# A hybrid Hyena and mLSTM encoder block on one core: where split weights lie, when pools are handed on, and what stands ahead of the first products

## The chip, the cores and the metric

The kernel runs on one core of a Trainium2 chip. The metric is device time in microseconds from launch to end, lower is better; the time before is the median of three runs, 2859.32 us (2859.23 to 2859.35).

## The reference, cut to what matters

All arrays are float32; L = 512 tokens, D = 2048, feed-forward width 5632.

```python
hn = rmsnorm(x, norm1_w)
proj = hn @ w_in                      # 2048 x 11280
conv_out = depthwise_conv3(proj[..., :5120])
y_a = hyena(conv_out[..., :3072])     # two long convolutions with learned filters
y_b = o * (mlstm_forward + mlstm_backward)
gate_a, gate_b = sigmoid(proj's last 4096 columns)      # "merge"
mixed = gate_a * (y_a @ w_branch_a) + gate_b * (y_b @ w_branch_b)
x = x + mixed @ w_out
gu = rmsnorm(x, norm2_w) @ w_gate_up  # 2048 x 11264
x = x + (silu(gu[..., :5632]) * gu[..., 5632:]) @ w_down
return rmsnorm(x, norm_f_w)
```

## The kernel before, in words

Every float32 operand of a product is split into two fp32r tiles, a high part (a cast on ScalarE) and the rest (a subtraction on VectorE). `mm3` (L78) makes one product of three TensorE instructions: high by high, high by rest, rest by high. A weight tile is the stationary operand in most stages.

Stages, in order of time: load and transpose x and the first column group of w_in (L302 to L348, to about 40 us); the other columns of w_in, with Hyena and mLSTM as a side stream between them (to 818 us); the merge gates (818 to 1138 us); branch a and branch b (to 1313 us); w_out (to 1495 us); gate_up (to 2376 us); down (to the end).

Merge and gate_up use one level of Strassen and Winograd (class `Winograd`, L1095): 256 columns are made by seven products with 256-column moving operands, over eight pairs of k blocks. `load` brings four raw tiles, `add` makes the eight sums s1 to s4, `split` the high and low tiles (14 splits for 256 columns, each used for four pairs, so by 12 instructions). Merge makes 16 such groups, gate_up 44. In merge the moving operands are the X blocks (pool `ap`) and their combinations T (pool `ts`); in gate_up all are T tiles (`tp`, `ta`, `tb`).

Merge's split weights go through a ring of six high and six low tiles: four in `wp` (names `wh`, `wl` in the trace) and two on the right side (`h`, `l`); its sums through six right-hand tiles. gate_up's go through five and five: four in `wp`, one in `h2` and `l2`. Laid out by the pools' sizes, the tiles of `wp`, the X blocks, `ts`, `h2` and `l2` start at multiples of 256 bytes; merge's right-hand `h` and `l` start 32 bytes below such a multiple, and all T tiles of gate_up 32 bytes above one (`shifted`, L58, is there for such offsets).

At the end of w_out the last 256 columns (`out_group(3, 1)`) are run to their end (L1410), then the pool `ap`, which holds the operand of w_out, is left (L1411), and the pools of gate_up take its place. The T tiles of pair 6 (`combos(b_a, ...)`, L1430) and the first products stand behind that in the code. gate_up's first group takes products 1 and 2 over pairs 0 to 6, then calls `late`, which transposes the last output columns and makes pair 7 from them (L1148 to L1156).

An x block is transposed on TensorE and split (L315 to L328). The first w_in tile is loaded after the first piece of x (L308 to L312). The side stream is made of generators: `hyena(q)` fetches its inputs when it starts (L833 to L835), unless the step before it has done so; `mlstm` does that only for a following `mlstm` (L974). In branch a, y_b and o are loaded by the SP queue (L1306). In down, the four first h tiles take the place of T tiles (`hpa`, L1463), and all raw h loads are issued ahead through three tiles (L1468).

The order of instructions on each engine is made by a planner, which goes by the order of the code, by what is ready and by estimated costs, so it is near the order of the code but not the same. Weight loads go through the SP queue.

```python
    def mm3(o, aH, aL, bH, bL, start, stop):
        mm(o, aH, bH, start, False)
        mm(o, aH, bL, False, False)
        mm(o, aL, bH, False, stop)
```

Of the kernel before, what the change touches and what calls it, by code (L numbers as in the profile page):

```python
# [8 lines left out]
F32 = mybir.dt.float32  # L9
# [25 lines left out]
def hybrid_block_kernel(ctx, tc, x, norm1_w, w_in, conv_w, conv_b, filt_w1, filt_b1, filt_freq1,  # L35
# [27 lines left out]
    ap_cm = tc.tile_pool(name="ap", bufs=32)  # L63
    ap = ap_cm.__enter__()
# [18 lines left out]
    def split(pool, tag, src, shape=(P, L)):  # L83
        h = new(pool, tag, shape, F32R)
        l = new(pool, tag, shape, F32R)
# [221 lines left out]
    raws = []  # L307
    for c, (c0, n) in enumerate(pieces):  # L308
        for tb in range(4):
            nc.sync.dma_start(xt[c][tb], x2d[tb * P:(tb + 1) * P, c0:c0 + n])  # L310
        if c in (0, 2, 3):
            raws.append(load_a(w_in, len(raws) * L, 0))  # L312
    first_group = group_feat(w_in, 0, KB, 0, X, raws)

    def x_block(kb):  # L315
# [3 lines left out]
        for tb in range(4):  # L319
            nc.tensor.transpose(ps[:, tb * P:(tb + 1) * P], xt[c][tb][:, k0:k0 + P], ident)  # L320
        return ps

    def x_split(kb, ps):
        h = new(ap, "a", dt=F32R)
        l = new(ap, "a", dt=F32R)
# [3 lines left out]

    for kb in range(0, KB, 2):  # L330
# [557 lines left out]
    def mlstm(h, following=None):  # L888
# [122 lines left out]
    def stream_a():  # L1011
        yield from gate_rows()
        yield from need("filter")
        for kind, n in (("hy", 0), ("hy", 1), ("hd", 0), ("hy", 2), ("hy", 3)):
            yield from hyena(n) if kind == "hy" else mlstm(n)
# [3 lines left out]
        for h in (1, 2, 3):  # L1019
            yield from mlstm(h, h + 1)  # L1020
# [74 lines left out]
    class Winograd:  # L1095
# [30 lines left out]
        def cols(self, c0, psf, loaded=None, after={}, late=None):  # L1126
# [35 lines left out]
            product(p3, s4, "22")  # L1162
# [64 lines left out]
    wm_cm = {t: tc.tile_pool(name="wm" + t, bufs=b, side="right", reuse_waits="tile") for t, b in (("r", 4), ("s", 6), ("h", 2), ("l", 2))}  # L1227
# [7 lines left out]
    def ring(tag, shape, dt, own, pool, extra, more):  # L1235
# [9 lines left out]

    merge = Winograd(
        w_in, XT, ring("wr", (P, 4, 256), F32, 3, wm["r"], "r", 4),
        ring("wh", (P, 4, P), F32R, 4, wm["h"], "h", 2), ring("wl", (P, 4, P), F32R, 4, wm["l"], "l", 2),
        lambda: new(wm["s"], "s", (P, 4, P)), xo, lambda: bt((P, 256)))
# [8 lines left out]
    def load_ya():  # L1258
        for b in range(8):
            ya.append(split(ap, "a", load_tile(d_ya, b, nc.gpsimd)))  # L1260
# [11 lines left out]
    for t in ("l", "h", "s", "r"):  # L1272
# [14 lines left out]
    def branch_a():  # L1287
# [3 lines left out]
        def put_yb():  # L1291
            t, o = raw.pop(0)
            nc.vector.tensor_tensor(t, t, o, ALU.mult)
            yb.append(split(py, "y", t))

        for g in range(8):
# [9 lines left out]
            raw.append((load_tile(d_yb, g, nc.sync), load_tile(d_o, g, nc.sync)))  # L1306
# [298 lines left out]
```

## Time and profile before

| what | value |
|---|---|
| median of three runs | 2859.32 us |
| the profiled execution's own time | 2869.02 us |
| its span, first to last instruction | 2867.3 us |
| TensorE (PE) busy | 2840.8 us, 99% |
| VectorE (DVE) busy | 2104.9 us, 73% |
| ScalarE (ACT) busy | 1273.0 us, 44% |
| GpSimd (POOL) busy | 186.2 us, 6% |

Busy means that at least one instruction of the engine was running. TensorE's instructions overlap: a product of 256 columns is shown as 0.28 us long, while the next one starts some 0.12 us later. The pace of a stretch is therefore read from the starts, or from the count of instructions in a window. In a tile's name, `T,wh` is the moving operand T with the stationary operand wh.

### The profile page before, as it was taken

Reading aid. Unit: us, or ns where it says so; the run is one execution under the profiler, and the core shown is the slowest. Engines: PE = TensorE matmul, PEld = TensorE weight load, DVE = VectorE, ACT = ScalarE, POOL = GpSimd, SP = SyncE. Lnnn points to the kernel's source line nnn. Section 1 sums busy time; section 2 is a strip of 40 time slices with the busy share of each in tenths; the row PEclk is TensorE's granted clock in tenths of the full one; section 3 lists DMA queues with packets and bytes.
Section 4 is the critical chain, followed back from the end, with each engine's and each line's share of the span. In section 5 each row is a group of like instructions: output and inputs, shape, how many; then the busy total and the mean of one; then the engine's idle time right before and its main releaser. Section 6 shows DMA issues by size and latency. Waiting matters only on the chain.

```text
span 2867.3 us, 47431 instructions
## 1 busy us (share of the span) xinstructions
PE 2840.8 (99%) x18028; PEld 2569.3 (90%) x18028; DVE 2104.9 (73%) x3844; ACT 1273.0 (44%) x2259; POOL 186.2 (6%) x431
## 2 busy tenths in 40 slices
PE   9999999999999999999999999999999999999998
PEld 7888878888899999888899999999999998888886
DVE  6898869888588888554459889888898885233336
ACT  5434453446645545223445444444444445233224
POOL 0101121012100001000010000000000000000000
PEclk9999999999999999999999999999999999999999
DMA  5334443344344445643443343334333336343433
GB/s 180 115 118 129 125 133 122 110 144 147 114 151 129 133 140 164 223 140 109 136 142 118 124 127 122 115 115 128 124 118 118 120 102 217 96 129 115 126 115 126
DMA packets 281490, 376.97 MB, mean 131 GB/s; under 512 B 18620, under 2 KB 214660, under 8 KB 281261
## 3 DMA queue, kind: packets, MB, share of 16 engines
q1 hardware_dynamic: 257243, 298.36, 34.0%
q0 software_dynamic: 22752, 73.44, 7.6%
q8 instruction: 141, 2.31, 0.3%
q10 hardware_dynamic: 1266, 2.13, 0.2%
q14 instruction: 88, 0.72, 0.1%
HBM read 326.67 MB, written 47.20 MB: 130 GB/s over the span
## 4 chain that ended last, share of the span: by engine, by line
PE 71%; DVE 1%; DMA 0%; ACT 0%; issue 0%; ACTq 0%
PE mm L76 50%; PE sd L76 21%; DMA wr<-in_w_down_dram 0%; PE sd L1364 0%; DVE h L87 0%; DVE T L1392 0%; DVE s L1122 0%; ACT h L86 0%; DVE wl L177 0%; DVE wl L1106 0%; PE sd L998 0%; DVE x L1532 0%; ACT sq L1535 0%; ACT x L1544 0%; DVE g L957 0%
## 5 line engine op out<-in xcount | busy, mean ns | idle before, releaser
L177 DVE TENSOR_TENSOR wl<-wr,wh 128x512 fp32r<-128x512 f32 x512 | 350.8, 689 | 452.8 <-ACT wh L176 444.7
L176 ACT CAST wh<-wr 128x512 fp32r<-128x512 f32 x512 | 316.7, 622 | 739.1 <-PE mm L76 674.3
L76 PE MATMUL mm<-a,wh 128*128 128x512 f32 (+1 forms) x2128 | 620.8, 375 | 0.4 <-ACT wh L176 0.4
L76 PEld LDWEIGHTS mm<-a,wh 128*128 128x128 f32 x2128 | 386.1, 189 | 67.5 <-ACT wh L176 0.8
L76 PE MATMUL mm<-T,wh 128*128 128x256 f32 x2232 | 401.2, 282 | 2.8 <-ACT T L1391 2.3
L76 PE MATMUL mm<-a,wl 128*128 128x512 f32 (+1 forms) x1064 | 398.2, 374 | 1.0 <-DVE wl L177 1.0
L76 PE MATMUL sd<-T,wh 128*128 128x256 f32 x2224 | 397.6, 281 | 0.0
L76 PE MATMUL mm<-wh,h 128*128 128x512 f32 x1280 | 394.7, 389 | 1.1 <-ACT h L86 1.1
L76 PEld LDWEIGHTS mm<-T,wh 128*128 128x128 f32 x2232 | 341.7, 189 | 3.4 <-ACT T L1391 2.5
L1105 ACT CAST wh<-s 128x512 fp32r<-128x512 f32 x365 | 226.8, 622 | 253.3 <-PE sd L76 123.5
L76 PEld LDWEIGHTS sd<-T,wh 128*128 128x128 f32 x2224 | 339.1, 188 | 0.0
L76 PE MATMUL mm<-T,wl 128*128 128x256 f32 x1116 | 311.8, 279 | 0.3 <-DVE wl L1106 0.3
L76 PE MATMUL sd<-T,wl 128*128 128x256 f32 x1112 | 310.0, 279 | 0.0
L76 PEld LDWEIGHTS mm<-wh,h 128*128 128x128 f32 x1280 | 240.3, 188 | 51.3 <-ACT h L86 1.3
L1106 DVE TENSOR_TENSOR wl<-s,wh 128x512 fp32r<-128x512 f32 x365 | 249.9, 686 | 11.5 <-ACT wh L1105 8.1
L76 PE MATMUL mm<-wl,h 128*128 128x512 f32 x640 | 249.1, 389 | 0.0
L76 PE MATMUL mm<-wh,a 128*128 128x512 f32 (+1 forms) x896 | 247.2, 360 | 0.0
L76 PEld LDWEIGHTS mm<-a,wl 128*128 128x128 f32 x1064 | 201.0, 189 | 35.8 <-DVE wl L177 1.4
L76 PEld LDWEIGHTS mm<-T,wl 128*128 128x128 f32 x1116 | 211.1, 189 | 0.5 <-DVE wl L1106 0.5
L76 PEld LDWEIGHTS sd<-T,wl 128*128 128x128 f32 x1112 | 209.8, 189 | 0.0
L76 PEld LDWEIGHTS mm<-wh,a 128*128 128x128 f32 x896 | 160.3, 189 | 24.6
L76 PE MATMUL mm<-wl,a 128*128 128x512 f32 (+1 forms) x448 | 161.0, 359 | 0.0
(368 smaller groups left out, 4776.3 us busy)
## 6 DMA issues: line engine op xcount, KB each, us to landing
wr<-in_w_in_dram SPq DMA_DIRECT2D x140, 512.0 KB, 3.6
r<-in_w_gate_up_dram SPq DMA_DIRECT2D x100, 512.0 KB, 4.6
wr<-in_w_down_dram SPq DMA_DIRECT2D x88, 512.0 KB, 3.7
wr<-in_w_gate_up_dram SPq DMA_DIRECT2D x76, 512.0 KB, 4.2
r<-in_w_in_dram SPq DMA_DIRECT2D x36, 512.0 KB, 4.5
wr<-in_w_out_dram SPq DMA_DIRECT2D x32, 512.0 KB, 3.6
d_h<-xo POOLq DMA_DIRECT2D x44, 256.0 KB, 2.6
hl<-d_h SPq DMA_DIRECT2D x44, 256.0 KB, 3.5
```

What stands on the lines that cost most here:

```text
L76: nc.tensor.matmul(o, a, b, start=start, stop=stop)
L176: nc.scalar.copy(h, src)
L177: nc.vector.tensor_tensor(l, src, h.bitcast(F32), ALU.subtract)
L1105: nc.scalar.copy(h, a)
L1106: nc.vector.tensor_tensor(l, a, h.bitcast(F32), ALU.subtract)
```

## The change

- The X blocks, y_a and the operand of w_out lie in two pools of eight tiles, `al` and `ah`, in place of `ap`; a tile holds high and low part of one block. The blocks 0 to 7 of w_out's operand lie in `ah`, 8 to 15 in `al`.
- Start: the first w_in tile is loaded in two halves, behind the first and the second piece of x. Six unread products of ones are put ahead of the first transposes, and two and six unread transposes between those of block 1.
- `mlstm(0)` fetches the inputs of `hyena(2)` ahead.
- Merge: the first two splits of each kind take tiles of `wp`, all others rings of five right-hand tiles; the sums take the eight `wh` and `wl` tiles of `wp`.
- y_b and o are loaded by the POOL queue in branch a.
- End of w_out: after four of the eight steps of the last group `ah` is left, gate_up's `ta`, `tb`, `r2` and `h2` take its place, and pair 6 is made; then the group is ended. gate_up's sums, three of its raw tiles and one low tile lie in tiles of `al`.
- gate_up's first group: products 1, 2 and 3 over pairs 0 to 3, then 4 and 5, then 6, then `late`, then pair 7 of all three. The second norm follows product 6 instead of product 3.
- Down: the first four h tiles and the raw h tiles lie in `al`; a raw h tile is loaded when an earlier one has been split.

```diff
-    ap_cm = tc.tile_pool(name="ap", bufs=32)
-    ap = ap_cm.__enter__()
+    al = ctx.enter_context(tc.tile_pool(name="al", bufs=8))
+    ah_cm = tc.tile_pool(name="ah", bufs=8, reuse_waits="tile")
+    ah = ah_cm.__enter__()
+
+    def block_tile(kb):
+        t = new(al if kb < 8 else ah, "a", (P, 2, L), F32R)
+        return t[:, 0, :], t[:, 1, :]
...
+        if c < 2:
+            nc.sync.dma_start(raws[0][:, 2 * c:2 * c + 2, :],
+                              w_in[2 * c * P:(2 * c + 2) * P, 0:256].rearrange("(k p) c -> p k c", p=P))
+        elif c < 4:
             raws.append(load_a(w_in, len(raws) * L, 0))
...
+    def idle(n, a=None):
+        for _ in range(n):
+            if a is None:
+                mm(unread[:, 0:P], onesf, onesf, True, True)
+            else:
+                nc.tensor.transpose(unread[:, 0:P], a, ident)
...
+            if kb == 1 and tb > 1:
+                idle((2, 6)[tb - 2], xt[c][tb][:, k0:k0 + P])
...
+    idle(6)
     for kb in range(0, KB, 2):
...
-            if n == 5 and ("qk", following) in done:
-                fetched_qk[following] = fetch_qk(following)
+            if n == 5 and following in done:
+                kind, m = following
+                if kind == "qk":
+                    fetched_qk[m] = fetch_qk(m)
+                else:
+                    fetched[m] = fetch(m, 0), fetch(m, 1)
...
-            else:
-                hl12 = {}
-                product(p1, a11, "11", pairs=range(7))
-                product(p2, a12, "21", hl12, range(7))
-                late()
-                product(p1, a11, "11", pairs=(7,))
-                product(p2, a12, "21", hl12, (7,))
...
-            product(p3, s4, "22")
+            if late is None:
+                product(p3, s4, "22")
+            else:
+                three = ((p1, a11, "11", {}), (p2, a12, "21", {}), (p3, s4, "22", {}))
+                for pairs in (range(4), (4, 5), (6,)):
+                    for ps, a, key, hl in three:
+                        product(ps, a, key, hl, pairs)
+                late()
+                for ps, a, key, hl in three:
+                    product(ps, a, key, hl, (7,))
...
-    wm_cm = {t: tc.tile_pool(name="wm" + t, bufs=b, side="right", reuse_waits="tile") for t, b in (("r", 4), ("s", 6), ("h", 2), ("l", 2))}
+    wm_cm = {t: tc.tile_pool(name="wm" + t, bufs=b, side="right", reuse_waits="tile") for t, b in (("r", 4), ("h", 5), ("l", 5))}
...
+    def sum_tile():
+        n_sum[0] += 1
+        return wtile("wh" if n_sum[0] % 2 else "wl", [P, 4, P], F32, 4)
...
+        def take():
+            n[0] += 1
+            if n[0] <= 2:
+                return wtile("w" + t, [P, 4, P], F32R, 4)
+            return new(wm[t], t, (P, 4, P), F32R)
...
-            raw.append((load_tile(d_yb, g, nc.sync), load_tile(d_o, g, nc.sync)))
+            raw.append((load_tile(d_yb, g, nc.gpsimd), load_tile(d_o, g, nc.gpsimd)))
...
-                mixed.append(split(ap, "a", t))
+                mixed.append(split(block_tile((len(mixed) + 8) % 16), t))
...
-    x2t_b = drive_last(out_group(3, 1))
-    ap_cm.__exit__(None, None, None)
...
+    last = out_group(3, 1)
+    for _ in range(4):
+        next(last)
+    ah_cm.__exit__(None, None, None)
...
+    TX += combos(b_a, w2["ta"])
+    x2t_b = drive_last(last)
+    low = [new(al, "a", (P, 2, L), F32R if n == 6 else F32) for n in range(8)]
...
-        G = gate_up.cols(f * P, mm_ps, *((first, {"22": second_norm}, last_pair) if f == 0 else ()))
+        G = gate_up.cols(f * P, mm_ps, *((first, {"2": second_norm}, last_pair) if f == 0 else ()))
...
-    hpa = ctx.enter_context(tc.tile_pool(name="hpa", bufs=8, reuse_waits="tile"))
+    h_first = [new(al, "a", (P, 2, L), F32R) for _ in range(4)]
+    h_raw.append(new(al, "a", (P, 2, L))[:, 0, :])
...
+        def load(k):
+            if k < nf:
+                nc.sync.dma_start(h_raw[k % 3], d_h[f0 + k])
```

## Rows read from the trace of the kernel before

**Rows 1.** The page: its first line and the engines' busy time.

```profile
span 2867.3 us, 47431 instructions
PE 2840.8 (99%) x18028; PEld 2569.3 (90%) x18028; DVE 2104.9 (73%) x3844; ACT 1273.0 (44%) x2259; POOL 186.2 (6%) x431
```

**Rows 2.** The waits of TensorE over the whole span, the three longest of its 14 rows: us in total, times, longest us.

```profile
PE sd L320 <- DMA xt<-in_x_dram: 6.3, 3, 4.1
PE mm L76 <- ACT T L1391: 2.3, 1, 2.3
PE sd L759 <- DMA g<-d_hy: 1.2, 1, 1.2
```

**Rows 3.** The timeline of TensorE in merge: the first instructions of a run with right-hand weights, of the next run with `wp` weights, and of the run after that (start us, us).

```profile
909.62 0.40 PE L76 MATMUL mm<-T,h 128*128 128x256 f32 x2
...
912.43 0.40 PE L76 MATMUL mm<-T,wh 128*128 128x256 f32 x2
...
918.18 0.40 PE L76 MATMUL sd<-a,h 128*128 128x256 f32 x2
```

**Rows 4.** Merge from its first to its last product, by stationary tile: `wh`, `wl`, `h`, `l` in this order (window, its length; busy us and, in brackets, instructions that touch the tile, by engine).

```profile
817.90:1137.80 319.90, 217.42 (x1200) 186.88 (x1201) 101.39 (x150) 92.93 (x150) 1.00 0.44 135
817.90:1137.80 319.90, 169.58 (x601) 115.02 (x600) 101.39 (x150) 1.00 0.44 135
817.90:1137.80 319.90, 105.54 (x592) 90.42 (x592) 50.25 (x74) 45.87 (x74) 1.00 0.44 135
817.90:1137.80 319.90, 83.09 (x296) 55.66 (x296) 50.25 (x74) 1.00 0.44 135
```

**Rows 5.** Busy time by window, all instructions: merge in its steady part and gate_up in its steady part (length; PE, PEld, DVE, ACT, POOL busy and, in brackets, instructions; granted clock; DMA share; GB/s).

```profile
840.00:1120.00 280.00, 280.00 (x2357) 280.00 (x2357) 245.91 (x438) 141.84 (x241) 17.28 (x32) 1.00 0.43 133
...
1700.00:2300.00 600.00, 600.00 (x5097) 600.00 (x5096) 539.50 (x943) 289.00 (x485) 17.30 (x32) 1.00 0.39 121
```

**Rows 6.** The same view where w_out goes over into gate_up: the whole stretch, and three parts of it with their granted clock.

```profile
1498.00:1514.00 16.00, 11.88 (x69) 10.58 (x69) 14.81 (x37) 12.16 (x30) 0.00 (x0) 0.79 0.19 59
1506.00:1508.00 2.00, 0.91 (x4) 0.69 (x4) 2.00 (x6) 1.58 (x3) 0.00 (x0) 0.53 0.00 0
1508.00:1512.00 4.00, 4.00 (x19) 4.00 (x20) 4.00 (x10) 3.20 (x6) 0.00 (x0) 0.50 0.25 72
1512.00:1514.00 2.00, 2.00 (x16) 2.00 (x15) 0.94 (x3) 0.62 (x1) 0.00 (x0) 0.76 1.01 326
```

**Rows 7.** The timeline there: the first product of gate_up, those with a wait (in brackets: idle before, and what ended it), and instructions whose lengths are used.

```profile
1495.21 0.40 PE L76 MATMUL mm<-T,wh 128*128 128x256 f32 x2
...
1502.11 0.28 PE L76 MATMUL mm<-T,wl 128*128 128x256 f32 x1
1504.64 0.38 PE L76 MATMUL mm<-T,wh 128*128 128x256 f32 x1 [2.25 <-ACT T L1391]
1505.50 0.39 PE L76 MATMUL mm<-T,wh 128*128 128x256 f32 x1 [0.48 <-DVE T L1392]
...
1507.09 0.80 PE L76 MATMUL mm<-T,h 128*128 128x256 f32 x2 [1.09 <-ACT h L1105]
```

**Rows 8.** VectorE and ScalarE in the same stretch: VectorE's busy time in a window, and instructions of three kinds: the scaled copy of a transposed block, the T cast, the T subtraction.

```profile
1496.00:1512.00 16.00, 15.86 (x40) 0.82 0.14 43
...
1499.75 0.69 ACT L1366 ACTIVATE bt<-sd,cols 128x512 f32<-128x512 f32 x1
1500.47 0.41 ACT L1391 CAST T<-bt 128x256 fp32r<-128x256 f32 x1
1496.69 0.75 DVE L1392 TENSOR_TENSOR T<-tt,T 128x256 fp32r<-128x256 f32 x2
```

**Rows 9.** TensorE's timeline at the start, transposes (L320) and first products, and, from another stage, an unread product's like: a float32 product of 128 columns (each is shown as two).

```profile
6.97 0.69 PE L320 MATMUL sd<-csm,xt 128*128 128x128 f32 x2 [1.23 <-DMA xt<-in_x_dram]
8.64 0.69 PE L320 MATMUL sd<-csm,xt 128*128 128x128 f32 x2 [0.99 <-DMA xt<-in_x_dram]
9.70 0.80 PE L76 MATMUL mm<-a,wh 128*128 128x512 f32 x1 [0.36 <-ACT wh L176]
...
12.28 1.20 PE L76 MATMUL mm<-a,wh 128*128 128x512 f32 x2
...
14.77 0.63 PE L76 MATMUL mm<-a,wh 128*128 128x512 f32 x2
...
1516.93 0.45 PE L76 MATMUL sd<-csm,rb 128*128 128x128 f32 x2
```

**Rows 10.** The fetch of `hyena(2)` on POOL and its wait on TensorE.

```profile
419.86 1.63 POOL L823 DMA_DIRECT2D g<-d_hy  x3
...
424.75 0.87 PE L759 MATMUL sd<-csm,g 128*128 128x128 f32 x6 [1.16 <-DMA g<-d_hy]
```

**Rows 11.** The change from gate_up to down: the last product of gate_up, the casts of the first h tiles, the first product of down.

```profile
2376.03 0.28 PE L76 MATMUL sd<-T,wl 128*128 128x256 f32 x1
...
2376.75 1.66 ACT L86 CAST h<-hl 128x512 fp32r<-128x512 f32 x3
...
2377.42 0.50 PE L76 MATMUL mm<-wh,h 128*128 128x512 f32 x1 [1.11 <-ACT h L86]
```

**Rows 12.** Waits on other engines: VectorE for loads of o in branch a, and ScalarE's casts in gate_up for TensorE (1600 to 2300 us).

```profile
DVE bt L1293 <- DMA bt<-d_o: 16.5, 6, 5.0
...
ACT wh L1105 <- PE sd L76: 144.2, 198, 0.8
```

More of the change, by code (lines that the diff above doesn't have):

```diff
@@ L81, in mm3, with split @@
         mm(o, aL, bH, False, stop)
-    def split(pool, tag, src, shape=(P, L)):
-        h = new(pool, tag, shape, F32R)
-        l = new(pool, tag, shape, F32R)
+    def split(tiles, src):
+        h, l = tiles
         nc.scalar.copy(h, src)
@@ L1014, in stream_a @@
         for kind, n in (("hy", 0), ("hy", 1), ("hd", 0), ("hy", 2), ("hy", 3)):
-            yield from hyena(n) if kind == "hy" else mlstm(n)
+            yield from hyena(n) if kind == "hy" else mlstm(n, ("hy", 2))
         ph_cm.__exit__(None, None, None)
@@ L1019, in stream_a @@
         for h in (1, 2, 3):
-            yield from mlstm(h, h + 1)
+            yield from mlstm(h, ("qk", h + 1))
     def stream_b():
@@ L1270, in hybrid_block_kernel @@
             nc.gpsimd.dma_start(dst[j], C[j])
-    for t in ("l", "h", "s", "r"):
+    for t in ("l", "h", "r"):
         wm_cm[t].__exit__(None, None, None)
@@ L1293, in put_yb @@
             nc.vector.tensor_tensor(t, t, o, ALU.mult)
-            yb.append(split(py, "y", t))
+            yb.append(split([new(py, "y", dt=F32R) for _ in range(2)], t))
         for g in range(8):
@@ new lines, in quarter, with in_turn, take @@
+    def quarter(t, dt=F32):
+        return (t.bitcast(F32) if dt == F32 else t).rearrange("p (k c) -> p k c", k=4)
+    sums2 = [quarter(low[n // 2][:, n % 2, :]) for n in range(6)]
+    raws2 = [new(w2["r2"], "r2", (P, 4, 256))]
+    raws2 += [t.bitcast(F32).rearrange("p b (k c) -> p (b k) c", k=2) for t in low[3:6]]
+    low2 = quarter(low[6][:, 0, :], F32R)
+    h_raw = [low[7][:, b, :].bitcast(F32) for b in range(2)]
+    def in_turn(order, tag, shape, dt, own, others):
+        n = [0, 0]
+        def take(half=0):
+            n[0] += 1
+            if order[(n[0] - 1) % len(order)]:
+                return wtile(tag, list(shape), dt, own)
+            n[1] += 1
+            return others[(n[1] - 1) % len(others)]
+        return take
@@ L1429, in hybrid_block_kernel @@
     first = gate_up.load(0)
-    TX += combos(b_a, w2["ta"])
     def last_pair():
@@ L1468, in load_h @@
     def load_h(f0, nf):
-        raw = []
-        for f in range(f0, f0 + nf):
-            t = new(hs, "hl")
-            nc.sync.dma_start(t, d_h[f])
-            raw.append(t)
-        H = {}
+        H = {}
+        def load(k):
+            if k < nf:
+                nc.sync.dma_start(h_raw[k % 3], d_h[f0 + k])
+        for k in range(3):
+            load(k)
         def get(k):
             if k not in H:
-                H[k] = split(hpa if f0 == 0 and k < 4 else hp, "h", raw[k])
+                if f0 == 0 and k < 4:
+                    tiles = h_first[k][:, 0, :], h_first[k][:, 1, :]
+                else:
+                    tiles = [new(hp, "h", dt=F32R) for _ in range(2)]
+                H[k] = split(tiles, h_raw[k % 3])
+                load(k + 3)
             return H[k]
@@ L1521, in hybrid_block_kernel @@
             for k in range(2):
-                W[(c, u + k)] = split(hp, "h", raw[:, k, :])
+                W[(c, u + k)] = split([new(hp, "h", dt=F32R) for _ in range(2)], raw[:, k, :])
     ssq3_c = new(cp, "ssq_c3", (P, 4, 4))
```

35 lines of the change are left out of this document (18 added, 17 removed).

## The prediction

> **What bounds the kernel now.** I read the page's first part: TensorE is busy 2840.8 of 2867.3 us [rows 1], so the end moves only by what TensorE loses: idle time, slow clock, or a slow pace between instructions that never wait. Idle time comes from the view of waits [rows 2]: at the start for x, where w_out goes over into gate_up, and once for a Hyena fetch. The rest is pace, which busy time hides. The windows give it by count: in gate_up 5097 instructions in 600 us, 117.7 ns each, in merge 2357 in 280 us, 118.8 ns each, both of 256 columns [rows 5]. The timeline splits merge's figure: a run of two splits with right-hand weights makes 24 instructions in 2.81 us (909.62 to 912.43), 117.1 ns each; the next four splits, from `wp`, 48 in 5.75 us, 119.8 ns each [rows 3], T being the moving operand in both.
>
> So three kinds of loss: a pace that goes with the place of the weights, a hole near 1500 us, smaller holes elsewhere.
>
> **Merge.** By layout the slow run has moving and stationary tiles at the same offset (both multiples of 256 bytes), the fast run weights 32 bytes below. In gate_up T lies 32 bytes above the weights of `wp`, the same distance, and the pace is 117.7 ns though the weights are in `wp` [rows 5]; so I take the distance, not the pool, as the cause. After the change `h` lies ten tiles of 2048 bytes below `r`, `l` ten below `h`, so both keep the 32 bytes, and `al`, `ah` and `ts` stay at multiples of 256. Of merge's 2688 products 1800 now have `wp` weights (1200 with `wh`, 600 with `wl`) [rows 4]. After it only two splits have, 24 products. So 1776 products gain 119.8 - 117.1 = 2.7 ns: 4.8 us. Bounds: 0, and 5.3 (3 ns each, as the starts are shown to 10 ns and a run's edges blur).
>
> The Trainium skill, "TensorE: Matmul & The Clock Gate", Part 2, step 1, says that moving operand and weight load read SBUF through two independent ports, so that loading the next weights takes nothing from the running product. By that rule this term is 0 and the sum 11.2. The trace disagrees within one stage, 117.1 against 119.8 ns, though it does not show why.
>
> The ring falls from six to five of each kind. While one split is used, four others are ready: 4 x 12 x 0.117 = 5.6 us for a cast and a subtraction. gate_up has such a ring of five; its casts do wait for TensorE to free a tile (144.2 us in 198 waits, 0.73 each [rows 12]), and TensorE keeps 117.7 ns. I take 0 for it. The sums go into tiles that no product reads; VectorE has 34 of 280 us free there [rows 5], and eight tiles replace six: 0.
>
> **From w_out to gate_up.** The stretch 1498 to 1514 us holds 69 TensorE instructions, 69 x 117.7 ns = 8.1 us of work in 16 us: 7.9 us lost [rows 6]. Products of pair 7 wait for T: 2.25, 0.48, then 1.09 us for the next split [rows 7]. Behind these waits the granted clock is 0.53 and 0.50, the lower of the two levels (1.2 GHz), and returns within 1512 to 1514 us [rows 6]: TensorE had idled before it fell and worked without a gap before it rose. About 4 us are waits, some 3 us the clock. The releasers are ScalarE and VectorE; VectorE is busy 15.86 of 16 us [rows 8], as pair 6, pair 7, six sums and the splits all fall there. The change does three things. (1) Pair 6 and `ta` stand after four of eight steps: seven T subtractions and five combinations at about 0.35 us (0.75 for two [rows 8]), 4 us of VectorE, move under the last four steps (96 products x 0.12 = 11.5 us). (2) The sums s1 to s4 lie in tiles of `al` that come free step by step, so most of six additions also go there. (3) Ahead of pair 7 stand 63 products, not 42: 7.4 us of cover in place of 4.9. Pair 7 needs the last columns, 8 transposes (0.9 us), two scaled copies (0.69 each), then seven casts and subtractions in turn (0.4 each): some 5 us to "22", 6 to "21". VectorE has for that stretch 12 such operations (4.2 us) and four split subtractions (2.8). That fits into 7.4 + 0.9 us, but narrowly, so I take 6.5 of 7.9 us. Bounds: 2.5 (only the longer cover, 21 x 117.7 ns) and 7.9. If the waits stay short, the clock term goes with them.
>
> The second norm moves behind product 6. Its squares are ready before, and product 7 and 4 (5.6 us) and the next group cover it: 0, bounds 0 and 1.1 us more (the wait in [rows 7] of that order).
>
> **Start.** Products of 512 columns take 0.43 us each at 12.28 (1.20 for two that overlap) and 0.23 at 14.77 (0.63 for two) [rows 9]: the lower level, then the full one. (The windows' clock column has no record before that.) The first product runs at 9.70; ahead of it stand only transposes with holes. Six unread float32 products (half-clock price twice 0.2 us, by the last of [rows 9], so 2.4 us) and eight unread transposes (0.35 us each at the lower level by the 8.64 row, 2.8 us) fill holes for DMA: the first before 4.06, the others between 5.7 and 8.6 us. If TensorE is at full clock by 9.70, then 4.8 us of half-clock work becomes 2.4: gain 2.4 us. The rest follows as x arrives ahead of need: between 15 and 36 us TensorE has no wait for x (all three waits of [rows 2] lie before 8.7). The first weights in halves: a 256 KB transfer less ahead of the second piece of x, and a cast that waited 0.36 us [rows 9]; I leave it at 0. Bounds: a loss of 0.5 (dummies delaying the first transposes), a gain of 3.0.
>
> **Hyena fetch.** Three loads issue at 419.86 and TensorE waits 1.16 us at 424.75 [rows 10]. Issued three units of `mlstm(0)` earlier, about 8 us, they land in time: 1.2 us. Bounds 0 (if no free tile) and 1.4.
>
> **gate_up to down.** The last product ends at 2376.3, the first of down starts at 2377.42 after waiting 1.11 us for the cast of h, which waits for T's tiles [rows 11]. The new h tiles were sums and raw weights, free before the last product: 1.1 us, bounds 0 and 1.2. Raw h loads issued one by one still run three ahead: 0.
>
> **POOL for y_b and o.** 16 issues at 0.54 us (1.63 for three [rows 10]) are 8.7 us on a queue that is busy 186 us in all [rows 1]; behind each stands the next load, and VectorE's product y_b x o waits for them. It waits now up to 5.0 us [rows 12] without TensorE noticing. Weight loads on SP lose these 16 from their way, but TensorE never waits for them. 0; bounds 0 and 5 us lost, if the last one is late for branch b.
>
> **Sum.** 4.8 + 6.5 + 2.4 + 1.2 + 1.1 = 16.0 us. The profiled execution took 2869.02 us (span 2867.3), 9.7 more than the median, with the same work; 2869.0 - 16.0 = 2853.0 there, and against the median 2859.3 - 16.0 = 2843.3 us.
>
> **Rivals.**
> 1. Pair 7 is late again: VectorE's queue holds the splits of the three interleaved products ahead of T. For it: 15.86 of 16 us busy [rows 8]. Against: pair 6 and sums have left. Only 2.5 of 6.5 is won: 12.0, 2847.3 us. Chance 0.20.
> 2. The dummies don't bring the clock up by 9.70, since holes remain between transposes as now. 0.3 in place of 2.4: 13.9, 2845.4 us. Chance 0.15.
> 3. Place makes no difference, the pace of [rows 3] having another cause (by the rule cited above): 11.2, 2848.1 us. Chance 0.08. The change would then not do what its first part says.
> 4. Two of these together, or the planner's new order opening holes of 6 us and more: 2854, no change. Chance 0.05.
> 5. Slower: in merge each of 222 right-hand splits comes late, as five tiles don't cover VectorE, which also makes the sums and waits for raw loads. It decides from 16.0 / 222 = 0.072 us a split; at 0.1 us it costs 22 and the end is 2865.5 us. Against: gate_up's ring of five [rows 5, 12]. Chance 0.05.
>
> **How the numbers follow.** The forecast, 2843.3, has 0.47; its own range is 2839 to 2847. Rivals 1 to 3 add 0.43 and lie below 2849. The range for 8 in 10 reaches from 2837 (all upper bounds together, 5.3 + 7.9 + 3.0 + 1.4 + 1.2 = 18.8, with a little more from a new order) to 2852, and leaves out rivals 4 and 5 and the edges. About 0.2%, 5.7 us, is what a measurement of this kernel can tell from no change. Faster by more than that (below 2853.6): 0.90 less 0.02 for edges, 0.88. Within: 0.05 + 0.02 = 0.07. Slower: 0.05.
>
> **What would show it.** Merge's window should hold 2688 products in about 315 us, with nearly all stationary tiles named `h` and `l`, and 117 ns in every run. Around the end of w_out no window should show a granted clock below 1.00, and waits for T should be under 1.5 us in all. The first products should stand 0.23 us apart at once. No wait for `g<-d_hy` near 420 us, none for `h` at the start of down. I am wrong if merge keeps 119.8 ns with `h` and `l`, if TensorE's waits list casts in merge, or if a hole at pair 7 remains with the clock at 0.50 behind it.

## The result and the profile after

The changed kernel takes 2867.91 us (median of 14 runs, 2863.22 to 2873.59); the kernel before, run beside it, 2860.79 us (14 runs, 2858.15 to 2868.93). The ratio is 1.0024, 95% interval 1.0016 to 1.0032: slower by about 7 us, where 16 us faster was forecast. Both kernels' runs spread by about 10 us (experiment 9 shows part of the reason), so single parts of the change are read from the traces and not from medians.

The profiled execution of the changed kernel took 2864.84 us. The page's first line and TensorE's busy time, which answer to [rows 1]:

```profile
span 2863.1 us, 47489 instructions
PE 2832.2 (99%) x18048; PEld 2558.9 (89%) x18048; DVE 2112.3 (74%) x3844; ACT 1267.7 (44%) x2255; POOL 195.3 (7%) x447
```

TensorE is busy 8.6 us less than before, and idle 30.9 us in place of 26.5. The waits of TensorE (us in total, times, longest), to be held against [rows 2]:

```profile
PE mm L83 <- ACT wh L182: 5.8, 3, 5.0
PE mm L83 <- ACT h L1131: 4.0, 1, 4.0
PE mm L83 <- DVE x L1584: 2.4, 1, 2.4
PE mm L83 <- ACT T L1439: 1.2, 1, 1.2
PE sd L83 <- DVE gb L502: 1.1, 1, 1.1
PE mm L83 <- DVE l L1132: 1.0, 1, 1.0
...
PE sd L340 <- DMA xt<-in_x_dram: 0.9, 2, 0.7
```

The wait for x has shrunk from 6.3 to 0.9 us, that for `g<-d_hy` is gone; two new waits of 4 and 5 us stand at the top.

To see where time went, every TensorE instruction of the one trace is set against the same instruction of the other, in the order of the program. The table gives how much later (+) the changed kernel got in each stretch (times of the kernel before):

| stretch, us | what | later by, us |
|---|---|---|
| 0 to 20 | start | -3.3 |
| 20 to 807 | w_in with the side stream | +0.5 |
| 807 to 827 | start of merge | +6.8 |
| 827 to 1148 | merge | -5.8 |
| 1148 to 1169 | branch a | +10.0 |
| 1169 to 1531 | w_out to gate_up | -4.6 |
| 1531 to 2372 | gate_up | -7.8 |
| 2372 to 2392 | gate_up to down | -1.4 |
| 2392 to 2816 | down | +1.5 |
| all | | -4.1 |

The last line agrees with the two profiled times (2864.84 - 2869.02 = -4.2). The 7.8 us in gate_up are no part of the change: by layout its T tiles keep their 32 bytes of distance from the weights, and e1 and e2, with the same gate_up as the changed kernel, go at the pace of the kernel before. They come from two paces that gate_up takes, the subject of experiment 9. Without them the change is 3.7 us slower.

**Start of merge.** The timeline (start us, us; in brackets idle before, and what ended it):

```profile
818.10 0.69 DVE L1148 TENSOR_TENSOR wh<-wr 128x512 f32<-128x512 f32 x1 [0.57 <-PE mm L83]
818.86 0.37 SPq L1140 DMA_DIRECT2D wr<-in_w_in_dram  x1
819.45 2.31 SPq L1140 DMA_DIRECT2D r<-in_w_in_dram  x4
824.25 0.62 ACT L1131 CAST h<-r 128x512 fp32r<-128x512 f32 x1 [6.95 <-DMA r<-in_w_in_dram]
824.92 1.32 PE L83 MATMUL mm<-a,h 128*128 128x256 f32 x4 [4.05 <-ACT h L1131]
```

The first column group needs the raw tile `r`. In SP's queue a load of `wr` for the second group stands ahead of it, and waits for a raw tile that a sum still reads. That sum goes into a `wh` tile, so it waits for a product of w_in's last columns (0.57 us, until 818.10). Only then `wr`, then `r` issue; `r` lands 4.8 us later.

**Branch a:**

```profile
1156.41 0.54 POOL L1302 DMA_DIRECT2D bt<-d_o  x1 [0.31 <-DVE y L93]
1162.92 0.69 DVE L1340 TENSOR_TENSOR bt<-bt,bt 128x512 f32<-128x512 f32 x1 [5.61 <-DMA bt<-d_o]
1163.70 0.62 ACT L92 CAST y<-bt 128x512 fp32r<-128x512 f32 x1 [7.78 <-DVE bt L1340]
1164.23 0.61 ACT L182 CAST wh<-wr 128x512 fp32r<-128x512 f32 x1
1164.90 1.22 PE L83 MATMUL mm<-a,wh 128*128 128x512 f32 x2 [4.96 <-ACT wh L182]
```

Read upwards: TensorE waits for a cast of weights. That cast has its data; it stands behind the cast of y on ScalarE, which waits for VectorE's product, which waits for o. The row of waits names ScalarE; the cause is a DMA three steps back.

The windows (length; busy us and instructions of PE, PEld, DVE, ACT, POOL; granted clock; DMA share; GB/s): merge and gate_up in their steady parts, branch a, w_out to gate_up:

```profile
840.00:1120.00 280.00, 280.00 (x2403) 280.00 (x2402) 254.99 (x448) 145.31 (x245) 17.92 (x34) 1.00 0.42 135
1700.00:2300.00 600.00, 600.00 (x5145) 600.00 (x5145) 544.73 (x951) 292.58 (x490) 17.35 (x32) 1.00 0.38 122
...
1152.00:1160.00 8.00, 7.11 (x28) 4.61 (x26) 4.49 (x8) 2.29 (x4) 3.23 (x6) 1.00 0.99 336
1165.00:1169.00 4.00, 4.00 (x10) 3.02 (x11) 2.64 (x5) 1.14 (x2) 1.62 (x3) 0.50 1.00 366
...
1512.00:1514.00 2.00, 0.77 (x3) 0.48 (x3) 1.63 (x5) 1.97 (x6) 0.00 (x0) 1.00 0.69 218
1516.00:1518.00 2.00, 2.00 (x12) 2.00 (x11) 2.00 (x6) 1.19 (x6) 0.00 (x0) 0.51 0.03 8
```

Merge makes 2403 instructions in 280 us where it made 2357 [rows 5]: 116.5 ns against 118.8. Behind the holes of branch a and gate_up the clock stands at its lower level (0.50 and 0.51), so that each costs more than its waits. Of the 10.0 us in branch a 5.1 are the hole itself and 2.4 the lower clock (twelve products start 0.43 us apart in place of 0.23, from 1164.9 to 1169.8 us); the rest are shorter waits for weights. And the last hole, at w_out to gate_up, is smaller but still there:

```profile
1511.49 1.27 ACT L1414 ACTIVATE bt<-sd,cols 128x512 f32<-128x512 f32 x2 [3.12 <-PE sd L1412]
1513.11 0.90 PE L83 MATMUL mm<-T,wh 128*128 128x256 f32 x2 [1.21 <-ACT T L1439]
```

The scaled copy begins as soon as the transposes have ended, and the products are through by then: nothing covers the way from the copy to T.

### The profile page after: what moved, and what is told of

It is laid out like the page before. It is cut to its first block, busy times and chain, and to the rows that moved or that the text cites. A ratio compares the mean times of both kernels' runs of the same rounds, so it can differ in the third digit from the quotient of the medians.

```text
span 2863.1 us, 47489 instructions
## 1 busy us (share of the span) xinstructions
PE 2832.2 (99%) x18048; PEld 2558.9 (89%) x18048; DVE 2112.3 (74%) x3844; ACT 1267.7 (44%) x2255; POOL 195.3 (7%) x447
## 4 chain that ended last, share of the span: by engine, by line
PE 68%; issue 2%; DMA 2%; DVE 1%; ACT 0%; POOL 0%; POOLq 0%; DVEq 0%; ACTq 0%; SPq 0%
PE mm L83 48%; PE sd L83 20%; DMA bt<-d_o 1%; DMA wr<-in_w_down_dram 0%; PE sd L1412 0%; DVE h L93 0%; DMA r<-in_w_in_dram 0%; DMA bt<-d_ya 0%; DVE bt L1340 0%; DVE wl L183 0%; POOL d_o L479 0%; POOL bt L1302 0%; ACT y L92 0%; DMA d_o<-st 0%; ACT h L92 0%
## 5 line engine op out<-in xcount | busy, mean ns | idle before, releaser
L83 PE MATMUL mm<-a,wh 128*128 128x512 f32 (+1 forms) x1808 | 564.0, 391 | 5.8 <-ACT wh L182 5.8
L83 PEld LDWEIGHTS mm<-a,wh 128*128 128x128 f32 x1808 | 336.3, 188 | 73.6 <-ACT wh L182 6.9
L83 PE MATMUL mm<-wh,h 128*128 128x512 f32 x1152 | 355.4, 389 | 0.0
L83 PE MATMUL mm<-a,wl 128*128 128x512 f32 x904 | 353.5, 391 | 0.4 <-DVE wl L183 0.3
L83 PE MATMUL mm<-T,wh 128*128 128x256 f32 x1976 | 352.4, 280 | 1.5 <-ACT T L1439 1.2
L83 PE MATMUL sd<-T,wh 128*128 128x256 f32 x1968 | 347.9, 279 | 0.0
L1131 ACT CAST wh<-a 128x512 fp32r<-128x512 f32 x371 | 230.8, 623 | 261.7 <-PE mm L83 118.7
L83 PEld LDWEIGHTS sd<-T,wh 128*128 128x128 f32 x1968 | 299.7, 188 | 0.0
L83 PE MATMUL mm<-wh,a 128*128 128x512 f32 (+1 forms) x1024 | 287.2, 364 | 0.6 <-DVE pp L418 0.6
L1132 DVE TENSOR_TENSOR wl<-a,wh 128x512 fp32r<-128x512 f32 x371 | 253.9, 689 | 38.7 <-ACT wh L1131 33.1
```

The lines of the kernel that those rows point to most:

```text
L83: nc.tensor.matmul(o, a, b, start=start, stop=stop)
L1131: nc.scalar.copy(h, a)
L1132: nc.vector.tensor_tensor(l, a, h.bitcast(F32), ALU.subtract)
```

## The experiments

Twelve runs; each is compared with the kernel before on the same chip, whose medians there were 2859.9 to 2860.7 us.

| run | median us | ratio to before (95%) |
|---|---|---|
| the changed kernel | 2867.91 | 1.0024 (1.0016 to 1.0032) |
| e1: y_b and o on SP | 2856.40 | 0.9991 (0.9979 to 1.0004) |
| e2: one raw load on POOL | 2860.48 | 1.0002 (0.9990 to 1.0015) |
| e3: late() earlier | 2862.50 | 1.0006 (0.9997 to 1.0015) |
| e4: all three | 2845.03 | 0.9946 (0.9932 to 0.9960) |
| e5: e4, weights at equal offset | 2854.05 | 0.9973 (0.9963 to 0.9984) |
| e6: e4, start as before | 2845.77 | 0.9943 (0.9931 to 0.9956) |
| e7: e4, no early fetch | 2847.88 | 0.9949 (0.9937 to 0.9961) |
| e8: e4, two products | 2845.17 | 0.9941 (0.9929 to 0.9953) |
| e9: e1 and e2 together | 2848.46 | 0.9969 (0.9956 to 0.9983) |
| e10: e5, 128 bytes apart | 2849.91 | 0.9962 (0.9948 to 0.9976) |
| e11: changed kernel, old merge | 2862.22 | 1.0005 (0.9993 to 1.0016) |
| e12: y_b, o and p on POOL | 2848.93 | 0.9957 (0.9944 to 0.9971) |

**1. The loads of y_b and o.**

```diff
-            raw.append((load_tile(d_yb, g, nc.gpsimd), load_tile(d_o, g, nc.gpsimd)))
+            raw.append((load_tile(d_yb, g, nc.sync), load_tile(d_o, g, nc.sync)))
```

> The changed kernel with one part undone: in branch a the loads of y_b and o are issued by SP again. Theory: the hole of the changed kernel at 1159.5 to 1170 us is made by that part (a load of o lands 6.5 us after its issue on POOL, VectorE's product waits 5.6 us for it, ScalarE's cast of y and behind it the cast of the next weights wait, TensorE idles 5.0 us and then runs at the lower clock for some 4 us). Then TensorE has no wait of over 1 us in branch a and the time falls by 9 to 10 us, to about 2858 (ratio 0.999). Rival A: the loads are late because of what all queues have to carry there (gate tiles, x tiles, weights), whichever queue issues them; then a hole of 5 us or more stays and the time changes by less than 3 us. Rival B: the 18 loads on SP push the weight loads back and a new wait for weights of over 2 us comes up.

Branch a has no wait of TensorE any more, and instruction by instruction the trace is 10.0 us earlier between 1148 and 1203 us than that of the changed kernel. Two of its windows there:

```profile
1150.00:1158.00 8.00, 8.00 (x37) 6.60 (x37) 5.68 (x9) 2.79 (x6) 0.00 (x0) 1.00 1.05 390
1158.00:1166.00 8.00, 8.00 (x37) 6.63 (x36) 4.99 (x8) 2.70 (x5) 0.00 (x0) 1.00 0.83 292
```

The theory holds; the DMA engines are about as full as in the changed kernel (share 0.87 against 0.92 over 1130 to 1170 us), so rival A falls, and no new wait for weights comes up.

**2. The order on SP.**

```diff
-                    nc.sync.dma_start(t, self.w[half][:, 4 * q:4 * q + 4, c0:c0 + 256])
+                    queue = nc.gpsimd if c0 == C_MA + 256 and half + q == 2 else nc.sync
+                    queue.dma_start(t, self.w[half][:, 4 * q:4 * q + 4, c0:c0 + 256])
```

> The changed kernel with one load of merge's second column group (the fourth raw tile, wr) issued by POOL in place of SP; nothing else. Theory: TensorE's wait of 4.05 us at the start of merge comes from SP's order: that wr load stands ahead of the first group's r load and waits for a raw tile that the sums free only after the last product of w_in has freed a wh tile. With it out of the way r is issued at about 807 us in place of 819.45, lands before 815, and the 6.8 us lost between 807 and 827 us shrink to 1.5 to 2.5 (the wait of 1.03 for l at 819.45 stays, since the sums still lie in tiles of the last w_in products); the time falls by 4.5 to 5.5 us. Rival: the place of the sums alone is the cause (VectorE's sums wait for wh tiles, the casts behind them); then r early changes nothing, and a wait of 3 us or more stays.

The timeline of this kernel:

```profile
806.30 2.04 SPq L1141 DMA_DIRECT2D r<-in_w_in_dram  x4
...
818.79 0.76 POOL L1141 DMA_DIRECT2D wr<-in_w_in_dram  x1 [1.46 <-DVE wh L1149]
...
819.15 0.39 PE L83 MATMUL mm<-a,l 128*128 128x256 f32 x1 [1.03 <-DVE l L1132]
```

`r` issues 13 us earlier, the same `wr` load still waits until 818.79, but alone, and only the wait of 1.03 us for `l` is left: 5.8 us won against the changed kernel at 842 us, of 6.8. So the place of the sums costs about 1 us by itself and the order on SP the rest.

**3. The transposes ahead of the products.**

```diff
                 for pairs in (range(4), (4, 5), (6,)):
+                    if pairs == (4, 5):
+                        late()
                     for ps, a, key, hl in three:
                         product(ps, a, key, hl, pairs)
-                late()
```

> The changed kernel with late() called after pairs 0 to 3 of the first three products of gate_up, ahead of pairs 4 to 6, in place of behind them. Theory: the hole that is left at 1511.6 us (waits 1.21 and 0.21, then the lower clock to 1517; 4.2 us lost) is there because on TensorE the eight transposes stand behind all 63 products, so no product covers the way from the transposes over copy, sums and casts to T. With 27 products behind them (3.2 us) TensorE's waits for T fall under 0.3 us, no window shows a clock below 1.00, and the time falls by 3 to 4.2 us. Rival: the sums of w_out's last columns (VectorE, ended at 1504.05) or VectorE's queue make T late; then the transposes wait in place of the products and 2 us or more stay lost.

TensorE has no wait there any more, and the trace is 3.5 us earlier behind it:

```profile
1506.00:1510.00 4.00, 4.00 (x37) 4.00 (x36) 3.49 (x6) 2.74 (x7) 0.00 (x0) 1.00 0.49 180
1510.00:1514.00 4.00, 3.90 (x33) 3.67 (x32) 3.78 (x11) 4.00 (x17) 0.00 (x0) 1.00 0.76 249
```

VectorE is still busy 3.49 and 3.78 of 4 us; that did not matter once products stood behind the transposes.

**4. The three together.** The three edits above in one kernel.

> The three edits above in one kernel: y_b and o on SP, one raw load of merge on POOL, late() after pairs 0 to 3. If the three holes are independent and the theories hold, the gains add up: 9.5 + 5 + 3.5 = 18 us less than the changed kernel, about 2850 us, a ratio of 0.996 to the kernel before. Rival: a hole that is filled only moves a stall to a later place; then it stands less than 10 us below the changed kernel.

The gains add up: 2845.03 us, 15 us less than the kernel before. Of the 22.9 us between its median and that of the changed kernel a part is gate_up's other pace (experiment 9). Its longest waits:

```profile
PE mm L83 <- DVE x L1586: 1.8, 1, 1.8
PE sd L83 <- DVE gb L502: 1.1, 1, 1.1
PE sd L340 <- DMA xt<-in_x_dram: 1.1, 3, 0.4
```

With the three holes out of the way the other parts bring nearly what the sum said (2843.3). That it comes so near is in part luck: `late()` ahead of pairs 4 to 6 is no part of the change that was predicted, and it alone brings 3.5 us in e3.

**5 and 10. Where merge's weights lie.**

```diff
-    wm = {t: cm.__enter__() for t, cm in wm_cm.items()}
+    wm = {"r": wm_cm["r"].__enter__()}
+    wmx_cm = shifted("wmx", 56, side="right")     # e10: 24 in place of 56
+    wm.update({t: wm_cm[t].__enter__() for t in ("h", "l")})
...
```

> The kernel of the three edits (e4_three) with one change of place: an unused tile of 224 bytes a partition ahead of merge's h and l, so that these weights lie at multiples of 256 bytes like the moving operands; nothing else. Theory (the distance between moving and stationary tile sets the pace): merge's 2664 products with h or l go at 119.9 ns as the wp weights of the kernel before did (rows 3), in place of 116.7 to 117.8 in the runs so far, so the time rises by 5.5 to 8.5 us, to about 2852. Rival (the pool or the tile's other neighbours were the cause, or two independent ports make place indifferent): merge keeps 117 to 118 ns and the time 2845.

> e5_equal with 96 bytes in place of 224 ahead of merge's h and l, so that the weights lie 128 bytes off a multiple of 256, the moving operands at multiples of 256. Theory A: any distance that is not a multiple of 256 bytes keeps merge at 116.7 to 117.8 ns; time 2845. Theory B: what counts is the place within 128 bytes (or a smaller power of two, from 64 on), where both lie equal again; then merge goes at 120.0 ns and the time is 2853 to 2854.

Merge's steady part in e4, in e5 and in e10:

```profile
840.00:1120.00 280.00, 280.00 (x2380) 280.00 (x2379) 253.63 (x441) 144.61 (x245) 17.35 (x32) 1.00 0.42 135
```

```profile
840.00:1120.00 280.00, 280.00 (x2335) 280.00 (x2335) 252.66 (x434) 139.18 (x236) 16.62 (x32) 1.00 0.41 133
```

```profile
840.00:1120.00 280.00, 280.00 (x2362) 280.00 (x2362) 252.78 (x438) 142.16 (x241) 17.31 (x32) 1.00 0.42 135
```

That is 117.6, 119.9 and 118.5 ns. The profiled run of e4 was the slowest of its five (2848.96 us); the changed kernel, e6 to e9 and e12, with the same tiles in merge, go at 116.5 ns. An unused tile of 224 bytes costs 9.0 us by the medians, about 2688 times the step from 116.5 to 119.9; the theory of e5 holds. For e10 neither theory does: 128 bytes lie between, so the pace is no matter of yes or no. Only three distances were tried. That it is the distance and not the place of the weights alone is borne out by gate_up, where the weights lie at multiples of 256 bytes, T 32 bytes above one, and the pace is 116.6 or 117.7 ns.

**6. The start.**

```diff
-    raws = [wp.tile([P, 4, 256], F32, tag="wr", name="wr_0", bufs=3)]
+    raws = []
...
-        if c < 2:
-
-            nc.sync.dma_start(raws[0][:, 2 * c:2 * c + 2, :],
-                              w_in[2 * c * P:(2 * c + 2) * P, 0:256].rearrange("(k p) c -> p k c", p=P))
-        elif c < 4:
+        if c in (0, 2, 3):
             raws.append(load_a(w_in, len(raws) * L, 0))
...
-                idle((2, 6)[tb - 2], xt[c][tb][:, k0:k0 + P])
...
-    idle(6)
```

> e4_three with the start as before: no unread products or transposes, the first w_in tile in one load behind the first piece of x. Theory: the first stage is 3.3 to 3.6 us later as in the comparison of the traces, of which 2.4 us are the clock (products of 0.43 us until 14.5 us) and about 1 us the halves, which let the first product start earlier; time 2848.5. Rival: the weights in halves carry it all and the clock would be up anyway; then the products behind 9.7 us take 0.23 us each at once and the time rises by at most 1.5 us.

Two rows of this kernel's timeline, the second product and those at 12.54 us:

```profile
9.70 0.78 PE L83 MATMUL mm<-a,wh 128*128 128x512 f32 x1
...
12.54 0.63 PE L83 MATMUL mm<-a,wh 128*128 128x512 f32 x2
```

Lower level until about 12.3 us, the full one behind that. In the changed kernel the first products go at the full level at once:

```profile
7.97 0.73 PE L83 MATMUL mm<-a,wh 128*128 128x512 f32 x2 [0.25 <-ACT wh L182]
...
10.33 0.63 PE L83 MATMUL mm<-a,wh 128*128 128x512 f32 x2
```

So the clock was not up anyway, as the rival had it; but at 40 us e6 is only 2.1 us behind e4, where 3.3 to 3.6 were expected, and the medians differ by 0.7, within the rival's bound. What the unread work and what the halves brought was not taken apart. The rest is not settled: in these two profiles the end of down differs by 2.5 us the other way with the same order of instructions there, where the wait for x is 0.9 us in e6 and 1.8 in e4, and merge goes at 116.5 ns in e6 and 117.6 in e4. Two us in one place can't be told apart by so few medians.

**7. The early fetch.**

```diff
-            yield from hyena(n) if kind == "hy" else mlstm(n, ("hy", 2))
+            yield from hyena(n) if kind == "hy" else mlstm(n)
```

> e4_three without the early fetch for hyena(2). Theory: the hole of 1.3 us at 423 us comes back, but the side stream falls back into the order of the kernel before too, and the waits that stand in the changed kernels at 452, 526 and 595 us (1.1, 0.7 and 0.7 us) go: the time changes by less than 1 us either way. Rival: those waits have nothing to do with the fetch; then it costs 1.2 to 1.4 us, as predicted for this part.

The wait for `g<-d_hy` is back (0.8 us), the gaps at 452, 526 and 595 us are gone, others of 1.2 and 0.9 us stand at 567 and 664 us, as in the kernel before (573 and 669 us); at 842 us the trace is 1.0 us behind e4, and the median is 2.9 higher. The theory is right on the order of the side stream; by the trace the fetch brings about 1 us, the theory's upper bound and near the rival's 1.2 to 1.4. How much of the 2.9 is its own stays open.

**8. Two products in place of three.**

```diff
-                three = ((p1, a11, "11", {}), (p2, a12, "21", {}), (p3, s4, "22", {}))
+                three = ((p1, a11, "11", {}), (p2, a12, "21", {}))
...
                 for ps, a, key, hl in three:
                     product(ps, a, key, hl, (7,))
+                product(p3, s4, "22")
```

> e4_three with only products 1 and 2 spread over the pairs of gate_up's first group (0 to 3, late(), 4 and 5, 6, then 7), product 3 whole behind them as in the kernel before; pair 6 and ta stay early. Theory: what counts is that products stand behind the transposes; 18 of them (2.1 us) are just enough for the 1.7 us from transposes to T, so the time rises by 0 to 1 us and no window there shows a clock below 1.00. Rival: the third product is what carries the gain; then a hole with a lower clock behind it comes back and 3 us or more are lost.

2845.17 against 2845.03 us, no wait of TensorE between 1490 and 1510 us and a granted clock of 1.00 throughout: 18 products behind the transposes do, and the third product brings nothing that can be measured.

**9. The two paces of gate_up.** e4 with the third edit taken back:

```diff
-                    if pairs == (4, 5):
-                        late()
                     for ps, a, key, hl in three:
                         product(ps, a, key, hl, pairs)
+                late()
```

> e4_three with late() back behind pair 6, as in the changed kernel; so y_b and o on SP and one raw load of merge on POOL, and the hole at the start of gate_up is there again (waits of 1.2 and 0.2 us, lower clock for some 3 us). So far the kernels with that hole (before, the changed one, e1, e2) had runs in two clusters 7 to 9 us apart, and in their profiles gate_up went at 117.78 or 116.67 ns throughout; the kernels without it (e3 to e8) had one cluster, and 116.67. Theory: gate_up's pace is settled where TensorE takes up work again after the hole, so this kernel has two clusters, at about 2848 and 2856 us, some 2 to 6 of 12 runs in the upper one. Rival: the upper cluster has to do with something else (chip, placement of the tiles in gate_up, which is the same in all of these); then all runs stand within 4 us about 2848.

Seven runs stand between 2846.79 and 2848.74, five between 2857.21 and 2859.46. The same two clusters are in the kernel before (ten and four of its 14 runs beside the changed kernel, 2858.15 to 2861.34 and 2866.99 to 2868.93). The 52 runs of the eight kernels without the hole (e3 to e8, e10, e12) have no second cluster; the widest, e3, spans 6.3 us. In the changed kernel's runs and in e11's (two of 12 above 2869 us) the gap is less clear. In the profile of e9 gate_up goes as in the changed kernel; in those of before [rows 5], e1 and e2 it goes slower, as in this row of e1:

```profile
1700.00:2300.00 600.00, 600.00 (x5097) 600.00 (x5096) 542.92 (x940) 288.88 (x485) 16.25 (x30) 1.00 0.38 121
```

5097 or 5145 instructions in 600 us, 117.7 or 116.6 ns, from the first to the last group, at the same granted clock. Over gate_up's 44 x 56 x 3 = 7392 products the difference is 8.1 us. The six profiles of kernels with the hole agree with this: three of runs in the upper cluster (before, e1, e2) have the slower pace, three in the lower one (changed kernel, e9, e11) the faster. How the hole leads to it is not shown.

**11. The old merge.** Pools, rings and sums of merge as before; all else as changed.

```diff
-    wm_cm = {t: tc.tile_pool(name="wm" + t, bufs=b, side="right", reuse_waits="tile") for t, b in (("r", 4), ("h", 5), ("l", 5))}
+    wm_cm = {t: tc.tile_pool(name="wm" + t, bufs=b, side="right", reuse_waits="tile") for t, b in (("r", 4), ("s", 6), ("h", 2), ("l", 2))}
...
-        split_tile("h"), split_tile("l"), sum_tile, xo, lambda: bt((P, 256)))
+        ring("wh", (P, 4, P), F32R, 4, wm["h"], "h", 2), ring("wl", (P, 4, P), F32R, 4, wm["l"], "l", 2),
+        lambda: new(wm["s"], "s", (P, 4, P)), xo, lambda: bt((P, 256)))
```

> The changed kernel with merge's pools, rings and sum tiles as in the kernel before (six high and six low tiles, four of each in wp; six right-hand sum tiles); all other edits stay, the holes in branch a and at the start of gate_up too. Theory: the merge edit as a whole brought 1776 x 3.2 ns = 5.6 us of pace and cost 5.8 to 6.8 us at merge's start, through the place of the sums, which also put the wr load ahead of r in SP's queue. Then the wait of 4 us at 820 us is gone, r is issued ahead of that wr, wp's weights go at 119.9 ns again, and the time stays within 2 us of the changed kernel's, runs with equal pace in gate_up compared (2864 and 2872). Rival: the wait at merge's start comes from the other edits (the early fetch moved the side stream, whose last tiles lie under r); then it stays and the time rises by 5 us.

The timeline of SP: `r` is ahead again.

```profile
794.39 11.47 SPq L1140 DMA_DIRECT2D wr<-in_w_in_dram  x3
806.08 2.04 SPq L1140 DMA_DIRECT2D r<-in_w_in_dram  x4
824.11 3.34 SPq L1140 DMA_DIRECT2D wr<-in_w_in_dram  x3
```

The wait of 4 us is gone, the trace is 7.1 us ahead of the changed kernel at 842 us (0.5 of it from before merge) and loses 5.4 of it again by 1127 us, 2357 instructions being made in merge's 280 us as before. So the merge edit as a whole costs a little more than it brings, and the order on SP comes with it, not with the fetch. Pools, rings and sums went back together, so which of them sets that order is not separated here.

**12. Why POOL was bad for y_b and o.**

```diff
-        nc.sync.dma_start(t, d_g[k][b])
+        nc.gpsimd.dma_start(t, d_g[k][b])
```

> e4_three with y_b and o on POOL as in the changed kernel, and the loads of the gate tiles p (d_g) on POOL too, so that y_b, o and p stand in one queue again and SP has the weights alone. In the changed kernel SP issues 14 gate tiles between 1134.3 and 1153.8 us and four more at 1157.8, as no y_b or o in its queue holds it back, and the DMA engines are full (share 0.99); in e1_yb_on_sp it issues 9 in that time. Theory: it is these early gate tiles (256 KB each, needed only groups later) that keep o from landing; in one queue with y_b and o they come in turn, TensorE's waits in branch a stay under 1 us in all, and the time is within 2 us of e4_three, 2845 to 2847. Rival: POOL's issue is the cause (0.54 us each, behind waits for VectorE and its other DMAs), or weights on a queue of their own crowd out o just as well; then waits of 3 us or more stay and the time is 2850 or more.

A wait of 2.5 us stays, for a weights' subtraction that VectorE makes behind the product that waits 3.9 us for o; against e4 4.4 us are lost by the traces in place of 10. Neither theory is met. With the gate tiles in one queue with o more than half of the loss is gone, as the theory has it; but the edit also moves them off SP, and what makes the other part (POOL's own queue, or weights that have SP alone) stays open.

## Why the prediction was wrong

It failed at two steps that were put at nothing, and a third was sized wrongly.

**"POOL for y_b and o ... 0; bounds 0 and 5 us lost."** It cost 10.0 us. [Rows 12] showed VectorE waiting up to 5.0 us for o "without TensorE noticing", and that was taken as slack. It was not followed to what is queued behind the waiting product: the cast of y, and behind it on ScalarE the cast of the next weights. Nor was it asked what hid those waits: weights split ahead. VectorE waits for o no longer in all than before (16.5 us over branch a in both kernels), and in e1 it waits 5.2 us at once without a wait of TensorE:

```profile
1148.64 0.69 DVE L1340 TENSOR_TENSOR bt<-bt,bt 128x512 f32<-128x512 f32 x1 [5.19 <-DMA bt<-d_o]
```

But there, counted from the traces in the order of the program, each cast of branch a's weights ends 1.4 us or more ahead of their first product (1.1 in the kernel before); in the changed kernel the three casts ahead of the hole end 0.05 to 0.7 us ahead. What was also not weighed: SP's waits for y_b and o had been holding back the gate tiles in the same queue. Freed of them, SP issued 14 gate tiles where e1 issued 9, into DMA engines that were full. By e12 that is a part of the cause and not all of it; and full engines alone are none, as e4 has a share of 0.98 over 1130 to 1170 us and no wait of TensorE there. In this kernel's DMA view (1130 to 1170 us: packets, MB, share of 16 engines) both queues move at once:

```profile
q1 hardware_dynamic: 4704, 6.82, 46.2%
q0 software_dynamic: 1768, 5.81, 45.0%
```

In e1 one queue has nearly all:

```profile
q1 hardware_dynamic: 7181, 10.47, 75.0%
q0 software_dynamic: 578, 1.87, 11.6%
```

The Trainium skill, "DMA: Bandwidth & Descriptors", section on queues, rings and completion order, says that each DMA engine takes turns between the queue rows that have work. The near equal shares do not speak against that, but they go with what is issued: in e12 they are 72.1% (POOL's queue) and 19.4%. No run here shows the turns themselves.

**"The sums go into tiles that no product reads ... 0."** True of merge, not of its start: the products of w_in's last columns still read those tiles. The direct cost is 1 us (e2); the other 5.8 came from SP's order, in which a load of the second group, freed by those sums, had been put ahead of `r` (e2; by e11 the order comes with the merge edit). The prediction looked at SP's queue for the weights in branch a only.

**"(3) Ahead of pair 7 stand 63 products ...: 7.4 us of cover."** On TensorE the transposes stand behind those 63 products, so the products cover what VectorE has left, not the way from the transposes to T. 4.6 us were won of the 6.5 forecast, and 3.5 more when `late()` moved (e3; 2.1 by the traces of e9 and e4): in all 6.7 to 8.1, where the upper bound was 7.9. Rival 1 named the hole, but laid it to VectorE's queue, which was not the cause.

**Merge's pace** was right in mechanism and low in size: 2688 x (118.8 - 116.5) = 6.2 us in place of 4.8 (the traces: 5.8). The 117.1 ns of [rows 3] came from a run of 24 instructions; 1800 products at 119.8 ns in a mean of 118.8 leave 116.8 for the others. Rival 3 is out: e5 alone loses 9.0 us by place. By the rule of the Trainium skill, "TensorE: Matmul & The Clock Gate", Part 2, step 1 (two independent read ports), place would be indifferent; the measurements, 119.9 against 117.6 ns, do not agree.

**Start, fetch, gate_up to down.** The clock was up with the first product, 2.1 to 3.3 us by the traces for 2.4. The wait for `g<-d_hy` went; of 1.2 us about 1 stayed (e7). The stretch of w_in as a whole is still 0.5 us later, and what took the rest was not found. gate_up to down brought 1.4 for 1.1. At the end of down 1.5 us were lost that no term had: the wait for x is 2.4 us there in place of 0.8, and between 0.9 and 2.9 us in the twelve runs. The ring of five never made TensorE wait in merge's steady part: rival 5 gave the right side for a wrong reason, and rival 4 (holes of 6 us and more from the new order) was nearest, at a chance of 0.05.

**The sum, closed.** By the traces, gate_up left out, the change is 3.7 us slower, where the forecast was 16.0 faster. Those 19.7 us are 10.0 (POOL), 6.8 (start of merge), 1.9 (pair 7), 1.7 (w_in, the fetch in it) and 1.5 (down), less 2.2 that merge, the start and gate_up to down brought beyond their terms.

**"9.7 more than the median, with the same work."** The work was the same; by its pace gate_up accounts for 8.1 of the 9.7 us. More runs of the changed kernel are long (7 of 14 above 2868.7 us, against 4 of 14 above 2866.9 before), which would make the medians differ by more (7.1 us) than the traces without gate_up (3.7); only one run of each was profiled, so this is argued and not shown.

## What to carry to other kernels

A wait that TensorE doesn't notice is slack only as far as split weights lie ahead: follow it through the in-order queue of each engine behind it, to the next cast of weights, before a transfer is moved. A load that waits in a queue also holds back what stands behind it, and moving it lets those go early, here into DMA engines that were full already. Products count as cover only if they stand behind the instruction whose result is awaited; and where split weights are loaded for every product, try where they lie against the moving operand: an unused tile of 224 bytes, which moved them to an equal place, cost 9 us here.

## What the runs showed of the hardware that was not expected

The pace of 256-column products goes with the distance of stationary from moving operand: 119.9 ns at an equal place within 256 bytes (e5), 118.5 at 128 bytes (e10), 116.5 or 117.6 at 32. The two values at 32 are the other surprise: with the same tiles a stage keeps one of two paces, 1.1 ns apart, to its end; gate_up took the slower one only in kernels where TensorE had a hole at its beginning; merge took it once (e4), though the wait of 1.0 us ahead of it stands in the kernels at 116.5 ns too. What sets it was not found.
